# Where layer B's modulation vectors are summed, and how many root series a linear-attention head runs

## The chip, the cores and the metric

The kernel runs on one core of one Trainium2 chip. The metric is the time of one execution on the device in microseconds (us); of several runs the median is taken. Of the engines this text speaks of TensorE (PE), VectorE (DVE), ScalarE (ACT), GpSimd (POOL) and of the queue of DMA issues on SyncE (SP). Each engine works through its own instructions in a fixed order.

## The reference, cut to what matters

Two layers work on 1024 tokens of width 1024. Layer A is a gated delta rule with 8 heads of 128, layer B a stick-breaking attention with 16 heads of 64 over keys and values that are computed once between the layers. Every layer, and the keys and values too, read the tokens through a norm that is modulated by vectors from a condition `c`:

```python
def _modulated_norm(x, gain, shift, scale):
    n = _rms(x, gain) * (1.0 + scale[:, None, :]) + shift[:, None, :]
...
    o = _chunk_gated_delta(q, k, v, g, beta)
    o = _rms(o, o_gain) * jax.nn.silu(z)
...
    o = jnp.concatenate(outs, axis=2).transpose(0, 2, 1, 3).reshape(B, T, W)
    o = o * jax.nn.silu(z)
    return o.astype(h.dtype) @ w_out
```

For each layer a 1024x3072 matrix `w_ada` multiplies the activated `c` and gives shift, scale and a gate for the layer's output (parts 0, 1 and 2); a 1024x2048 matrix does the same for the keys and values (shift and scale). These are products of a matrix with one vector: little arithmetic, but 4 MB of weights for each part.

## The kernel before

**Stages.** From 0 to 80 us the kernel loads `x`, sums layer A's own shift and scale and projects the first heads. From 80 to some 680 us it runs layer A's 8 heads. The loop over heads (L748 to L775) emits for each head the projection and convolution of the next head's q and k, the finishing of a modulation part that is pending (`pend`), the values, the triangular solve, and `stage_c`, which runs the chunk recurrence and norms the output. The out-projection's first part begins at 640 us, its rest and the keys (`keys_values`, first half) run to 829.65 us, the values half from there to some 920 us, and layer B with its attention and out-projection to the end.

**Projections.** Each float32 weight tile is cast to a high part `whi` (ACT, L211), the rest `wlo` is taken by a subtract (DVE, L212), and three matmuls (L116 to L118) multiply high by high, high by low and low by high. These matmuls fill PE's order between everything else.

**Modulation vectors.** `mod_acc` (L145) sums a 512-wide half of a part: 8 loads of 256 KB from `w_ada` (SP, L151), and on DVE one product (L153) and 7 multiply-adds (L155) of 128x512, which leave a tile of 128 partial sums for each column. `mod_fin` (L170), in its turned form, transposes that tile on PE (four 128x128 transposes `pc` for a half, L182), sums each transposed block by an ACT instruction with accumulation (L185), adds the bias, and writes shift, scale or, after one more transpose `pr` (L202), the gate's row to memory. In the loop over heads the list `mods` (L527) gives each of the heads 0 to 5 one part: layer A's gate, scale and shift of the keys and values, then scale, shift and gate of layer B.

**The output's norm.** At the end of `stage_c` (L726 to L744) each half of the tokens has its own root series on DVE: a sum of squares by ACT, `qe`, `so`, then `rsqrt` (L96 to L101, 11 instructions on 128x4), a multiply of the 128x512 tile `osb`, four PE transposes `pto`, a multiply by the silu gate `sz`, and a store.

**Keys and values.** `kv_half` runs 16 times (8 blocks of columns n, two halves of the tokens), four steps each; a step is 24 matmuls of 128x256. n from 0 to 3 makes keys, n from 4 to 7 values, so the values half has 32 steps. After each n, `mod_b(n)` (L919) loads 128 rows of the normed tokens, applies layer B's scale and shift on ACT (L923), casts on DVE (L926) and subtracts on POOL (L927), which makes the tiles `hbT` that layer B's projections read.

**Order.** Up to the keys and values stage a scheduler orders all engines by its own plan. In the keys and values stage PE's order is that in which the code emits (`manual_schedule`, L947), and the other engines are still ordered by the scheduler. Loads are issued on SP in its order, and wait there for a free buffer.

Of the kernel before, what the change touches and what calls it, by code (L numbers as in the profile page):

```python
# [8 lines left out]
F32 = mybir.dt.float32  # L9
# [3 lines left out]
ALU = mybir.AluOpType  # L13
# [9 lines left out]
def kernel(  # L23
# [146 lines left out]
    def mod_fin(pool, ps_pool, ps_tag, i, part, accs, j0=0, turned=False):  # L170

        t = pool.tile([P, ND], F32, name="mt", tag="mt", bufs=2)
# [27 lines left out]
        else:  # L200
# [326 lines left out]
    mods = [(0, 2), (2, 1), (2, 0), (1, 1), (1, 0), (1, 2)]  # L527
# [160 lines left out]
    def stage_c(h, st):  # L688
# [37 lines left out]
        for hf in range(TH):  # L726
            cs = slice(hf * 4, hf * 4 + 4)
            osb = osbs[hf]
            so = gp.tile([P, 4], F32, name="so", tag="so")
            for i in range(4):  # L730
                sqo = gp.tile([P, P], F32, name="sqo", tag="sqo")
                S.activation(out=sqo, in_=osb[:, i], func=AF.Square, accum_out=so[:, i:i + 1])

            qe = gp.tile([P, 4], F32, name="qe", tag="qe")
            V.tensor_scalar(out=qe, in0=n2[:, 0, cs], scalar1=EPS, scalar2=EPS * P, op0=ALU.add, op1=ALU.mult)
            V.scalar_tensor_tensor(out=so, in0=so, scalar=1.0 / P, in1=qe, op0=ALU.mult, op1=ALU.add)
            ro = rsqrt(gp, so, 4, "ro")
            V.tensor_tensor(out=osb, in0=osb, in1=ro[:, :, None].broadcast_to([P, 4, P]), op=ALU.mult)
            pt = ch_pool.tile([P, 4, P], F32, name="pto", tag="ch")
            for i in range(4):  # L740
                PE.transpose(pt[:, i], osb[:, i], ident)
            V.scalar_tensor_tensor(out=szs[hf], in0=pt.rearrange("p a b -> p (a b)"), scalar=ogain,
                                   in1=szs[hf], op0=ALU.mult, op1=ALU.mult)
            dma(out=oTa[h, :, hf * 512:hf * 512 + 512], in_=szs[hf])  # L744
# [4 lines left out]
    for h in range(HA):  # L749
# [23 lines left out]
        if h < len(mods):  # L773
            i, part = mods[h]
            pend = (i, part, [mod_acc(gp, i, part, n0, 512, 2) for n0 in (0, 512)])  # L775
# [143 lines left out]
    def mod_b(n):  # L919
# [360 lines left out]
```

## Time and profile before

| | us |
|---|---|
| median of 3 runs | 1466.41 (1465.34 to 1467.45) |
| profiled execution | 1462.12 |
| its span, first to last instruction | 1460.3 |
| PE busy | 1374.8 |
| DVE busy | 1040.8 |
| ACT busy | 760.6 |
| POOL busy | 92.3 |

The profiled execution lies 4.3 us under the median, and 1.8 us of it are outside the span. PE's matmuls overlap and their ends are modelled, so a busy PE says only that something is queued; times at which PE sits idle and stretches at a lower granted clock say more. The granted clock is a share of 2.4 GHz; its lower level is 1.2 GHz.

### The profile page before, as it was taken

The numbers are of one execution on the slowest core, as the hardware profiler recorded it, in microseconds if no ns is written. First come the engines' busy times: TensorE is split into PE (matmuls) and PEld (weight loads), VectorE is DVE, ScalarE is ACT, GpSimd is POOL, SyncE is SP. The second block draws the span as 40 slices with busy tenths as digits, with TensorE's granted clock in tenths as the row PEclk, the third lists the DMA queues.
The fourth block names the chain that finished last, engine by engine and source line by source line (L and its number), as shares of the span: only waits on it lengthen the run. The fifth ranks groups of instructions, "written<-read, shape, count | busy, mean of one in ns | idle before, by whom it ended". The sixth has DMA issues, their size and how long they took to land.

```text
span 1460.3 us, 23391 instructions
## 1 busy us (share of the span) xinstructions
PE 1374.8 (94%) x8603; PEld 1145.8 (78%) x8603; DVE 1040.8 (71%) x2459; ACT 760.6 (52%) x1614; POOL 92.3 (6%) x98
## 2 busy tenths in 40 slices
PE   4989999799999999999799999999999999998998
PEld 3567778578878777788689999788888888885676
DVE  3568698878778788954886610488888888989332
ACT  5656546446564646431784422366666666665110
POOL 1000000000000000000221011301011011000000
PEclk9999999799999999999999999999999999999999
DMA  9334324443444444444844433624233233234511
GB/s 316 107 107 124 89 51 120 123 137 84 142 108 133 108 137 134 148 127 162 301 160 159 160 131 116 181 73 116 54 101 106 69 105 87 84 84 131 174 59 56
DMA packets 168132, 181.15 MB, mean 124 GB/s; under 512 B 36617, under 2 KB 121426, under 8 KB 168018
## 3 DMA queue, kind: packets, MB, share of 16 engines
q1 hardware_dynamic: 165184, 171.17, 39.4%
q0 software_dynamic: 2432, 8.39, 1.6%
q8 instruction: 68, 1.11, 0.3%
q14 instruction: 46, 0.38, 0.1%
q10 hardware_dynamic: 402, 0.10, 0.0%
HBM read 140.22 MB, written 39.40 MB: 123 GB/s over the span
## 4 chain that ended last, share of the span: by engine, by line
PE 70%; DVE 18%; ACT 6%; DMA 3%; issue 2%; SPq 0%; ACTq 0%; DVEq 0%
PE pj L116 16%; PE pj L117 16%; PE pj L118 16%; DVE kp L1074 3%; PE ptw L1089 3%; PE pa L1114 2%; PE pa L1115 2%; PE pl L1069 1%; PE pl L1068 1%; PE pgr L576 1%; DVE qk L515 1%; DVE wl L1096 1%; DVE macc L155 1%; DMA mraw<-in_w_ada_dram 1%; PE pa L1111 1%
## 5 line engine op out<-in xcount | busy, mean ns | idle before, releaser
L118 PE MATMUL pj<-hT,wlo 128*128 128x512 f32 x496 | 203.0, 410 | 10.2 <-DVE wlo L212 10.2
L116 PE MATMUL pj<-hT,whi 128*128 128x512 f32 x496 | 205.4, 414 | 3.7 <-ACT qk L513 2.6
L117 PE MATMUL pj<-hT,whi 128*128 128x512 f32 x496 | 204.5, 412 | 0.0
L1074 DVE TENSOR_TENSOR_SCAN kp<-kp,stick 128x896 f32<-128x896 f32 (+7 forms) x128 | 179.1, 1401 | 3.9 <-ACT kp L1070 2.6
L1070 ACT ACTIVATE kp<-pl,nrq 128x512 f32<-128x512 f32 (+1 forms) x192 | 107.0, 580 | 48.6 <-PE pl L1069 39.9
L1094 ACT ACTIVATE wh<-ptw 128x512 fp32r<-128x512 f32 (+3 forms) x152 | 84.6, 557 | 67.4 <-PE ptw L1089 63.2
L118 PEld LDWEIGHTS pj<-hT,wlo 128*128 128x128 f32 x496 | 95.2, 192 | 27.6 <-DVE wlo L212 11.8
L116 PEld LDWEIGHTS pj<-hT,whi 128*128 128x128 f32 x496 | 95.2, 192 | 24.2 <-issue 3.7
L116 PE MATMUL pj<-hbT,whi 128*128 128x512 f32 x256 | 108.0, 422 | 0.0
L117 PEld LDWEIGHTS pj<-hT,whi 128*128 128x128 f32 x496 | 95.3, 192 | 15.8
L116 PE MATMUL pj<-wo,oh 128*128 128x512 f32 x256 | 103.8, 405 | 4.0 <-ACT oh L254 2.3
L117 PE MATMUL pj<-wo,oh 128*128 128x512 f32 x256 | 102.1, 399 | 0.0
L118 PE MATMUL pj<-wo,ol 128*128 128x512 f32 x256 | 101.3, 396 | 0.5 <-DVE ol L255 0.5
L117 PE MATMUL pj<-hbT,whi 128*128 128x512 f32 x256 | 101.2, 395 | 0.0
L118 PE MATMUL pj<-hbT,wlo 128*128 128x512 f32 x256 | 101.2, 395 | 0.0
L1089 PE MATMUL ptw<-ident,kp 128*128 128x128 f32 x576 | 91.6, 277 | 8.1 <-DVE wl L1096 5.5
L212 DVE TENSOR_TENSOR wlo<-wraw,whi 128x1024 fp32r<-128x1024 f32 x56 | 68.7, 1226 | 39.8 <-ACT whi L211 35.5
L211 ACT CAST whi<-wraw 128x1024 fp32r<-128x1024 f32 x56 | 59.1, 1055 | 72.1 <-PE pj L117 61.0
L1096 DVE SCALAR_TENSOR_TENSOR wl<-ptw,wh 128x512 fp32r<-128x512 f32 (+1 forms) x140 | 87.3, 624 | 8.1 <-ACT wh L1094 7.2
L1089 PEld LDWEIGHTS ptw<-ident,kp 128*128 128x128 f32 x576 | 68.4, 142 | 27.3 <-DVE wl L1096 12.0
L1114 PE MATMUL pa<-wh,vt 128*128 128x256 f32 (+1 forms) x280 | 78.5, 302 | 10.6 <-DVE o L1131 10.6
L116 PE MATMUL pj<-whi,hkT 128*128 128x256 f32 x256 | 73.2, 286 | 2.4 <-DVE x L265 1.6
(324 smaller groups left out, 3428.8 us busy)
## 6 DMA issues: line engine op xcount, KB each, us to landing
mraw<-in_w_ada_dram SPq DMA_DIRECT2D x96, 256.0 KB
wraw<-in_w_in_a_dram SPq DMA_DIRECT2D x32, 512.0 KB
mraw<-in_w_ada_kv_dram SPq DMA_DIRECT2D x32, 256.0 KB
xr<-x_dram SPq DMA_DIRECT2D x16, 512.0 KB
wraw<-in_w_kv_dram SPq DMA_DIRECT2D x16, 512.0 KB
kT_dram<-kt SPq DMA_DIRECT2D x32, 256.0 KB
wraw<-in_w_in_b_dram SPq DMA_DIRECT2D x16, 512.0 KB
Kh<-kT_dram SPq DMA_DIRECT2D x32, 256.0 KB
```

The costliest lines, as they stand in the source:

```text
L116: PE.matmul(ps, lh, rh, start=start, stop=False)
L117: PE.matmul(ps, lh, rl, start=False, stop=False)
L118: PE.matmul(ps, ll, rh, start=False, stop=stop)
L211: (copy or S.copy)(out=hi, in_=raw)
L212: (eng or G).tensor_tensor(out=lo, in0=raw, in1=hi, op=ALU.subtract)
L1070: S.activation(out=kp[:, s0:s0 + sw], in_=pl[:, :sw], func=AF.Sigmoid, scale=nrq[p][:, t, e:e + 1])
L1074: V.tensor_tensor_scan(out=kr, data0=kr, data1=stick[:, T - n:][:, ::-1], initial=1.0, op0=ALU.mult, op1=ALU.max)
L1089: PE.transpose(pt[:, i], kps[p, e, 2 * g + q][:, j * P:(j + 1) * P], ident)
L1094: S.activation(out=wh[:, :nb], in_=pt[:, :nb], func=AF.Copy, bias=-1.0)
L1096: V.scalar_tensor_tensor(out=wl[:, :nb], in0=pt[:, :nb], scalar=-1.0, in1=wh[:, :nb], op0=ALU.add, op1=ALU.subtract)
L1114: PE.matmul(dst, lh, wh[:, sl], start=(j == 0), stop=False)
L1115: PE.matmul(dst, lh, wl[:, sl], start=False, stop=(j == nj - 1))
```

## The change

It has four parts.

1. `mods` is cut to layer A's gate and the keys' and values' scale and shift. Each of the heads 0 to 5 sums one half (8 DVE instructions, 8 loads) where it summed a whole part, and a part is finished after every second head.
2. Layer B's three parts are summed in the values half, in 12 quarters of 256 columns. A quarter (`mod_quarters`) has 4 loads of 256 KB into a ring of five buffers `x2k`, which the keys' tiles `kt` use as well, and 8 DVE instructions of 128x256. They are emitted at the steps of `MOD_Q`, and the column sums (two transposes `pc` on PE, two accumulations on ACT, small DVE rows) four steps later. The gate's transpose `pr` follows the last of them.
3. `mod_b` is emitted at the steps of `MOD_B`, where it followed each n, and its subtract moves from POOL to DVE.
4. `stage_c` runs one root series of 8 columns for both halves, in the heads 0 to 6; the last head keeps two.

```diff
+    def mod_quarters(pool, i, part):
+        for n0 in range(0, D, 256):
+            src = mod_src[i][:, part * D + n0:part * D + n0 + 256].rearrange("(p k) n -> p k n", k=8)
+            acc = pool.tile([P, 256], F32, name="macq", tag=("of", "oh", "ol")[n0 // 256 % 3], bufs=2)
+            for k in range(0, 8, 2):
+                raw = pool.tile([P, 2, 256], F32, name="mrawq", tag="x2k", bufs=5)
+                dma(out=raw, in_=src[:, k:k + 2])
+                for kk in range(2):
+                    if k + kk == 0:
+                        V.tensor_scalar(out=acc, in0=raw[:, 0], scalar1=cact[:, 0:1], scalar2=None, op0=ALU.mult)
+                    else:
+                        V.scalar_tensor_tensor(out=acc, in0=raw[:, kk], scalar=cact[:, k + kk:k + kk + 1], in1=acc,
+                                               op0=ALU.mult, op1=ALU.add)
+            yield acc, n0 // P
...
-    mods = [(0, 2), (2, 1), (2, 0), (1, 1), (1, 0), (1, 2)]
+    mods = [(0, 2), (2, 1), (2, 0)]
+    half_acc = []
...
-        for hf in range(TH):
-            cs = slice(hf * 4, hf * 4 + 4)
...
-            ro = rsqrt(gp, so, 4, "ro")
...
+        groups = [(0, 1)] if h < HA - 1 else [(0,), (1,)]
+        for group in groups:
...
+            ro = rsqrt(gp, so[:, ga], 4 * len(group), f"ro{len(group)}")
+            for hf in group:
...
-        if h < len(mods):
-            i, part = mods[h]
-            pend = (i, part, [mod_acc(gp, i, part, n0, 512, 2) for n0 in (0, 512)])
+        if h < 2 * len(mods):
+            i, part = mods[h // 2]
+            half_acc.append(mod_acc(gp, i, part, h % 2 * 512, 512, 2))
+            if h % 2:
+                pend, half_acc = (i, part, half_acc), []
...
-            G.tensor_tensor(out=hT[hf][:, 1, n], in0=xs, in1=hT[hf][:, 0, n], op=ALU.subtract)
+            V.tensor_tensor(out=hT[hf][:, 1, n], in0=xs, in1=hT[hf][:, 0, n], op=ALU.subtract)
...
+    def mods_b(step, made):
+        if quarters and quarters[0][0] + 4 <= step:
+            _, i, acc, j0 = quarters.pop(0)
+            mod_fin(kp_, wk_pool, "wk", 1, (1, 0, 2)[i], [acc], j0, tg if i == 2 else None, turned=True)
+        if step in MOD_Q:
+            n = MOD_Q.index(step)
+            quarters.append((step, n // 4, *next(made)))
...
+                    if n >= 4:
+                        mods_b(step, made)
+                        if step in MOD_B:
+                            mod_b(MOD_B.index(step))
+                        step += 1
...
-            mod_b(n)
...
+    MOD_Q = (0, 1, 3, 4, 6, 7, 9, 10, 16, 19, 22, 25)
+    MOD_B = (15, 16, 18, 19, 21, 22, 24, 26)
```

Three places show what it does to the engines' orders. DVE first, before, a piece of head 1's solve: `ttmp` and `tt` are the pair of small instructions that a row of the triangular solve takes, `macc` is the summing of a modulation part, `vv`, `Sn` and `so` belong to the head before.

```order
L606 TENSOR_TENSOR tt<-tt,ttmp 128x2x24
L709 TENSOR_SCALAR vv<-pw,b_1132 128x128
L603 TENSOR_TENSOR ttmp<-bf,tt 128x3x23
L155 SCALAR_TENSOR_TENSOR macc<-mraw,cact,macc 128x512
L606 TENSOR_TENSOR tt<-tt,ttmp 128x3x23
L717 SCALAR_TENSOR_TENSOR Sn<-Sn,gA_110,pS 128x128
L603 TENSOR_TENSOR ttmp<-bf,tt 128x3x22
L515 SCALAR_TENSOR_TENSOR qk<-xp,ccol,qk 128x1024
L606 TENSOR_TENSOR tt<-tt,ttmp 128x3x22
```

DVE, the same piece of head 1's solve in the changed kernel.

```order
L623 TENSOR_TENSOR tt<-tt,ttmp 128x2x24
L620 TENSOR_TENSOR ttmp<-bf,tt 128x3x23
L726 TENSOR_SCALAR vv<-pw,b_1132 128x128
L623 TENSOR_TENSOR tt<-tt,ttmp 128x3x23
L620 TENSOR_TENSOR ttmp<-bf,tt 128x3x22
L623 TENSOR_TENSOR tt<-tt,ttmp 128x3x22
L734 SCALAR_TENSOR_TENSOR Sn<-Sn,gA_110,pS 128x128
L620 TENSOR_TENSOR ttmp<-bf,tt 128x3x21
L228 TENSOR_TENSOR wlo<-wraw,whi 128x1024
```

Between the first `ttmp` of head 1 and the end of its solve the kernel before has 14 rows of `macc`; the changed kernel has none there, since the part's second half was summed earlier and the next part begins with head 2. A `wlo` row of the next weights, which stood behind the solve, now stands within it.

PE in the changed kernel, at step 29 of the values half (the steps count from 0), where the gate's last column sums are taken. `macq` is the last quarter, `tg` the gate's vector.

```order
L117 MATMUL pj<-kwl,hkT 128x256
L118 MATMUL pj<-kwh,hkT 128x256
L198 MATMUL pc<-ident,macq 128x128 x2
L218 MATMUL pr<-ident,tg 8x128
L116 MATMUL pj<-whi,hkT 128x256
L117 MATMUL pj<-wlo,hkT 128x256
```

Twelve such pairs `pc` now stand in the values half among the projections' matmuls, and this last one has `pr` right behind it, which reads what ACT and DVE make of the pair.

SP in the changed kernel, at the end of the keys half and the start of the values half. `kt` are tiles of keys that are stored, `mrawq` the quarters' loads, `wraw` weights of keys and values.

```order
L941 DMA kT_dram<-kt 128x512 x8
L177 DMA mrawq<-in_w_ada_dram 128x2x256 x5
L233 DMA wraw<-in_w_kv_dram 128x4x256
L177 DMA mrawq<-in_w_ada_dram 128x2x256
L233 DMA wraw<-in_w_kv_dram 128x4x256
L177 DMA mrawq<-in_w_ada_dram 128x2x256 x2
L941 DMA kT_dram<-kt 128x512 x3
```

The quarters' loads stand around the next weights' loads and around the last stores of keys, where the kernel before had the weights and the stores alone.

## Rows read from the trace of the kernel before

**Rows 1.** The page: busy time, share of the span, instructions

```profile
PE 1374.8 (94%) x8603; PEld 1145.8 (78%) x8603; DVE 1040.8 (71%) x2459; ACT 760.6 (52%) x1614; POOL 92.3 (6%) x98
```

**Rows 2.** Windows of layer A: stretch, its length, each engine's busy us, PEclk, DMA

```profile
core 0: us, PE busy (x) PEld busy (x) DVE busy (x) ACT busy (x) POOL busy (x), PEclk, DMA share, GB/s
...
256.00:284.00 28.00, 17.89 (x68) 12.83 (x67) 27.11 (x102) 12.81 (x32) 0.00 (x0) 0.70 0.47 129
284.00:373.00 89.00, 87.97 (x631) 71.15 (x630) 62.51 (x196) 50.80 (x134) 0.00 (x0) 1.00 0.43 117
...
460.00:484.00 24.00, 21.02 (x104) 17.11 (x103) 23.85 (x77) 17.99 (x36) 0.00 (x0) 0.93 0.51 148
...
514.00:560.00 46.00, 44.23 (x240) 36.33 (x240) 43.73 (x159) 24.75 (x55) 0.00 (x0) 1.00 0.43 129
```

**Rows 3.** Waits of PE from 256 to 284 us: total, times, longest

```profile
PE pj L118 <- DVE wlo L212: 5.4, 1, 5.4
PE pgr L576 <- ACT kdec L549: 3.2, 2, 1.6
```

**Rows 4.** Chain of waits from 254 to 284 us: start, length, what

```profile
254.80 0.66 DVE macc L155
...
259.16 3.02 DMA mraw<-in_w_ada_kv_dram
...
263.93 0.66 DVE macc L155
...
274.85 1.15 DVE wlo L212
276.04 0.79 PE pj L118
276.83 3.57 PE pgr L576 x8
280.40 0.43 PE pj L116
```

**Rows 5.** Instructions on the sums' tile: count, ns min/median/max, first and last start

```profile
L155 DVE SCALAR_TENSOR_TENSOR macc<-mraw,cact,macc x84: 735/744/755, 93.5 to 543.4; 128x512 f32<-128x512 f32 x84
...
L182 PE MATMUL pc<-ident,macc x48: 270/272/330, 221.6 to 572.2; 128*128 128x128 f32 x48
L185 ACT ACTIVATE macc<-pc x48: 268/278/331, 222.2 to 573.3; 128x128 f32<-128x128 f32 x48
...
L153 DVE TENSOR_SCALAR macc<-mraw,cact x12: 472/481/487, 91.9 to 529.5; 128x512 f32<-128x512 f32 x12
```

**Rows 6.** Timeline of PE around one group of column sums: start, length

```profile
221.31 0.40 PE L118 MATMUL pj<-hT,wlo 128*128 128x512 f32 x1
221.55 0.60 PE L182 MATMUL pc<-ident,macc 128*128 128x128 f32 x4
221.91 0.48 PE L116 MATMUL pj<-hT,whi 128*128 128x512 f32 x1
222.22 0.40 PE L117 MATMUL pj<-hT,whi 128*128 128x512 f32 x1
```

**Rows 7.** Windows of the values half

```profile
840.00:860.00 20.00, 20.00 (x173) 20.00 (x173) 3.65 (x5) 5.85 (x10) 2.66 (x2) 1.00 0.49 162
860.00:880.00 20.00, 20.00 (x173) 20.00 (x172) 2.35 (x4) 5.73 (x10) 3.63 (x2) 1.00 0.38 116
```

**Rows 8.** Windows of the two stretches with the highest DMA rate

```profile
0.00:20.00 20.00, 4.71 (x16) 2.99 (x17) 8.02 (x32) 13.04 (x21) 4.17 (x20) 1.00 0.90 323
700.00:720.00 20.00, 14.94 (x76) 11.90 (x75) 17.68 (x43) 18.57 (x46) 6.47 (x9) 0.91 0.96 335
```

**Rows 9.** Groups of DVE instructions from 80 to 700 us: busy us, mean ns

```profile
L587 DVE TENSOR_TENSOR qk<-qk,gb 128x512 f32<-128x512 f32 x16 | 10.9, 682 | 0.0
...
L101 DVE SCALAR_TENSOR_TENSOR ro_y<-ro_z,ro_y 128x4 f32<-128x4 f32 x48 | 7.5, 156 | 0.4
```

**Rows 10.** Issues of the sums' loads on SP

```profile
L151 SPq DMA_DIRECT2D mraw<-in_w_ada_dram x64: 327/328/702, 82.0 to 539.9; - x64
```

More of the change, by code (lines that the diff above doesn't have):

```diff
@@ L168, in mod_rows, with mod_fin @@
         return row
-    def mod_fin(pool, ps_pool, ps_tag, i, part, accs, j0=0, turned=False):
-        t = pool.tile([P, ND], F32, name="mt", tag="mt", bufs=2)
+    def mod_quarters(pool, i, part):
[12 more added lines that the diff above has]
+            yield acc, n0 // P
+    def mod_fin(pool, ps_pool, ps_tag, i, part, accs, j0=0, t=None, turned=False):
+        t = t if t is not None else pool.tile([P, ND], F32, name="mt", tag="mt", bufs=2)
         nj = accs[0].shape[1] // P
@@ L199, in mod_fin @@
                                    op0=ALU.add, op1=ALU.mult)
-        else:
+        elif js.stop == ND:
             pr = ps_pool.tile([P, 512], F32, name="pr", tag=ps_tag)
@@ L724, in stage_c @@
             osbs.append(osb)
-        for hf in range(TH):
-            cs = slice(hf * 4, hf * 4 + 4)
[L728 to L736, printed above, removed]
-            ro = rsqrt(gp, so, 4, "ro")
[L738 to L744, printed above, removed]
@@ new lines, in stage_c @@
+        so = gp.tile([P, NC], F32, name="so", tag="so")
+        qe = gp.tile([P, NC], F32, name="qe", tag="qe")
+        groups = [(0, 1)] if h < HA - 1 else [(0,), (1,)]
+        for group in groups:
+            ga = slice(group[0] * 4, group[-1] * 4 + 4)
+            for hf in group:
+                for i in range(4):
+                    sqo = gp.tile([P, P], F32, name="sqo", tag="sqo")
+                    S.activation(out=sqo, in_=osbs[hf][:, i], func=AF.Square, accum_out=so[:, hf * 4 + i:hf * 4 + i + 1])
+            V.tensor_scalar(out=qe[:, ga], in0=n2[:, 0, ga], scalar1=EPS, scalar2=EPS * P, op0=ALU.add, op1=ALU.mult)
+            V.scalar_tensor_tensor(out=so[:, ga], in0=so[:, ga], scalar=1.0 / P, in1=qe[:, ga], op0=ALU.mult,
+                                   op1=ALU.add)
+            ro = rsqrt(gp, so[:, ga], 4 * len(group), f"ro{len(group)}")
+            for hf in group:
+                osb = osbs[hf]
+                r = ro[:, (hf - group[0]) * 4:(hf - group[0]) * 4 + 4]
+                V.tensor_tensor(out=osb, in0=osb, in1=r[:, :, None].broadcast_to([P, 4, P]), op=ALU.mult)
+                pt = ch_pool.tile([P, 4, P], F32, name="pto", tag="ch")
+                for i in range(4):
+                    PE.transpose(pt[:, i], osb[:, i], ident)
+                V.scalar_tensor_tensor(out=szs[hf], in0=pt.rearrange("p a b -> p (a b)"), scalar=ogain,
+                                       in1=szs[hf], op0=ALU.mult, op1=ALU.mult)
+                dma(out=oTa[h, :, hf * 512:hf * 512 + 512], in_=szs[hf])
@@ L926, in mod_b, with sums_of_mods @@
             V.tensor_copy(out=hT[hf][:, 0, n], in_=xs)
-            G.tensor_tensor(out=hT[hf][:, 1, n], in0=xs, in1=hT[hf][:, 0, n], op=ALU.subtract)
+            V.tensor_tensor(out=hT[hf][:, 1, n], in0=xs, in1=hT[hf][:, 0, n], op=ALU.subtract)
+    tg = kp_.tile([P, ND], F32, name="tg", bufs=1)
+    quarters = []
+    def sums_of_mods():
+        for part in (1, 0, 2):
+            yield from mod_quarters(kp_, 1, part)
+    def mods_b(step, made):
[5 more added lines that the diff above has]
+            quarters.append((step, n // 4, *next(made)))
     def keys_values():
-        parts, tail = kv_weights(0), None
+        parts, tail, made, step = kv_weights(0), None, sums_of_mods(), 0
         yield
```

## The prediction

> **What bounds the kernel now.** I began with the page's busy times: PE is busy for 94% of the span and DVE for 71% [rows 1]. So most of the time is PE's, and work taken from DVE is worth something only where PE waits for DVE. The windows of layer A show where that is [rows 2]. From 284 to 373 us PE is busy for 87.97 of 89 us, DVE for 62.51: less DVE work gives nothing there. From 256 to 284 us it is the other way round: DVE 27.11 of 28 us, PE 17.89, and the granted clock is 0.70, so some of the stretch ran at 1.2 GHz, the lower level. From 460 to 484 us there is a smaller place of the kind, with PE at 21.02 of 24 and a clock of 0.93, and from 514 to 560 us PE lacks 1.77 us. The waits name the releaser: one wait of 5.4 us for `wlo`, which DVE makes, and 3.2 us for `kdec`, which ACT makes from what DVE gives it [rows 3]. The chain of waits goes through DVE's queue from 254.80 to 276 us: five pieces of `macc` (the first at 254.80, the last at 263.93, each 0.66), a wait of 3.02 us for a load `mraw` in between, then at 274.85 the `wlo` for which PE waits [rows 4]. The sums of modulation parts are on the path there.
>
> The values half looks the other way. PE is busy for 20.00 of 20 us, DVE for 3.65 and 2.35, and the DMA engines for 0.49 and 0.38 of their time [rows 7]. DVE and the queues have room, and PE has none: each instruction that is put into PE's order there costs its whole length.
>
> **Part by part.** *DVE work that leaves layer A.* 96 instructions sum there now, 84 of 0.744 us and 12 of 0.481 [rows 5], and half of them go: 42 x 0.744 + 6 x 0.481 = 34 us. Besides, one root series of 8 columns takes the place of two of 4: with `qe` and `so`, 13 of 156 ns from start to end [rows 9] in layer A's loop leave for each of seven heads, about 1 us a head when they follow each other at some 0.075 us. Most of that hides under PE and is worth nothing. What counts:
>
> The first wall, 256 to 284 us. PE is idle for 28 - 17.89 = 10.1 us, and the matmuls that run at the lower clock cost more: 8 `pgr` in 3.57 us, of which half is lost, 1.8, and the `pj` at 0.43 us [rows 4] against the 0.23 from start to start at full clock [rows 6], 0.2 each for four or five of them, 0.9. At most 10.1 + 2.7 = 12.8 us can come back. From the order: in head 1's solve 14 `macc` leave, at 0.66 us each by the chain's pieces 9.2 us, and 1 us of root rows; in their place an `e` row and some `nm` rows move in, some 2.5 us. So DVE's part gets 7.7 us shorter. At the low end the clock falls all the same and other waits take 2 us of it: 6. I take 10, since a DVE queue that is 7.7 us shorter leaves only some 2.5 us of idle time, nearer to the second wall, where 3 us of idle time cost a clock of only 0.93 [rows 2]. What is late next is PE's own queue.
>
> The second wall, 460 to 484 us: 24 - 21.02 = 3.0 us idle and about 1 us of clock. Half of the `macc` of that head leaves, 8 x 0.66 = 5.3 us, and I take 3, with 1 and 4 as bounds. 514 to 560 us and short waits elsewhere: 1.77 us idle; I take 1.5, bounds 0 and 3.
>
> *PE work that leaves layer A.* A group of four transposes lets the next matmul start 221.91 - 221.55 = 0.36 us later, and the one behind it 0.31 after that where 0.23 is the rule [rows 6]: 0.44 us. Three parts have six groups: 2.6 us, and `pr` once, 0.2: 2.8 in all (2.5 to 3). The ACT accumulations, 24 of 0.278 [rows 5], lie beside PE's work. Layer A together: -10 - 3 - 1.5 - 2.8 = **-17.3 us** (-9.5 to -23).
>
> *PE work that enters the values half.* 12 pairs of transposes. Two transposes less than a group leave 0.44 - 0.22 = 0.22 us at the lowest, a whole group's 0.44 is the highest; I take 0.33: 4.0 us (2.6 to 5.3). The last pair has `pr` right behind it in an order that is fixed. PE must wait for the pair's end, 0.27 [rows 5], two accumulations of 0.28 with their reads of the sum, some 0.2 each, 1.0 together, and the bias row on DVE, some 0.16 by the small rows [rows 9], before `pr` can run, itself as long as one of the pair, 0.27: 1.2 to 2.0 us with nothing ahead on ACT, and up to 4 if a cast of 1 us or two is queued there. I take 1.8. Together **+5.8 us** (3.8 to 9.3).
>
> *DVE, SP and POOL in the values half.* 84 multiply-adds and 12 products of 128x256: by the line through 156 ns for 4 columns and 744 for 512 [rows 5, 9] about 0.45 us each, 42 us; 16 subtracts of 0.68 [rows 9], 11 us. DVE uses 3.65 us of 20 [rows 7], so 53 us in 90 fit. The sums stand before `wlo` and `kwl` rows in DVE's queue, and a late load holds those up; the weights' ring is a whole n, 22 us, ahead. Without this cover each late row would cost PE its lateness. 48 issues on SP at 0.33 us [rows 10] are 16 us. `mod_b` moved later still ends before 911 us by its last step, 26; PE needs `hbT` from some 920. POOL loses its 16 subtracts, for which nobody waits there. All this at nothing, if the loads come in time; that is the first rival.
>
> Sum: -17.3 + 5.8 = **-11.5 us**, from the profiled 1462.1 to 1450.6. The profiled run lies 4.3 us under the median; on the median that is 1466.4 - 11.5 = **1455**.
>
> **Rivals.** *The values half becomes bound by its loads (slower).* A step is 24 matmuls, at 173 in 20 us [rows 7] 2.78 us. Eight quarters, 8 x 4 x 256 KB = 8.4 MB, must be summed before PE reaches the transposes of the eighth, after 15 steps and 7 pairs: 43.4 us from the half's start. Other traffic in that time is 139 GB/s by the mean of the windows [rows 7], 6 MB, less 1 MB of `mod_b` loads that move out. 13.4 MB in 43.4 us are 310 GB/s, just under the two highest stretches of the trace, 323 and 335 [rows 8]. So it can go wrong. At 280 GB/s the eighth quarter comes 4.5 us late, at 250 10 us, and PE, in a fixed order, waits for all of it; the saving of 11.5 is gone at 244 GB/s, and below some 232 the kernel is slower by over 3 us; at 225 it stands at 1471. For it: five buffers, on which stores of keys wait too. Against it: with 3.02 us for a load [rows 4] and 0.9 for its two DVE rows five buffers turn over 1.3 MB in 3.9 us, 335 GB/s, where the quarters ask for 195; and the sums may start before the half does, since the order has five loads ahead of it. The Trainium skill's page "DMA: Bandwidth & Descriptors", section "Anatomy of one DMA — SWDGE (gpsimd) path", gives some 2.0 us for each transfer and its bytes at 436 GB/s besides, so by my estimate from it 13.4 MB take 31 us and this rival falls away, with the sum as it stands; the trace's highest windows of 323 and 335 GB/s do not reach that rate, and the page's fit is of another issuing queue. Chance 0.12, most of it slower.
>
> *The wall only moves.* Layer A's orders come from a plan. If the joint root series, whose second half must wait for the first's squares and whose `pto` come together, or the earlier `wlo` row put another wait in front of PE, the first wall gives 3 instead of 10 and the second nothing: -3 - 1.5 - 2.8 + 5.8 = -1.5, 1465, no measurable change. For it: the wall's chain also has `vT`, `qk`, `n` and `sz` rows, which stay. Against it: DVE's whole load falls in the very stretch in which it is full. Chance 0.10.
>
> *The wall goes altogether,* and the clock with it: -12.8 - 4 - 3 - 3 = -22.8, + 5 for the values half: -17.8, 1449. Chance 0.13.
>
> **How the numbers follow.** The forecast has 0.65. A difference of 0.2%, 2.9 us, is about what a measurement tells from no change. Two of its larger terms at their far ends give 1450 and 1463, all of them at once 1447 and 1466; the first rival reaches past 1469. The range 1446 to 1466 takes in all but the worse half of the first rival and what no bound here covers. Faster takes the forecast, the third rival and a little of the second: 0.80. Same: most of the second and the mild end of the first: 0.11. Slower: the rest of the first: 0.09.
>
> **What would show it.** Right: the stretch from the first `ttmp` of head 1 to its end with PE idle for under 4 us, and a granted clock near 1.00; layer A shorter by 14 to 20 us; in the values half PE without idle time but for one wait of 1 to 2 us before `pr`, and the half longer by about 6. Wrong: waits of `pc` for `macq` with a DMA as releaser behind them, or a DMA share under 0.9 while they last (then the ring, not the rate, binds); a wait of PE for `wlo` or `osb` of 5 us in another head; `hbT` later than PE's first read of it.

## The result and the profile after

| | us |
|---|---|
| kernel before, median of 4 runs | 1466.93 (1465.34 to 1469.04) |
| changed kernel, median of 4 runs | 1448.68 (1445.75 to 1453.10) |
| ratio, 95% interval | 0.988 (0.986 to 0.990) |
| profiled execution before / after | 1462.12 / 1449.83 |
| span before / after | 1460.3 / 1448.1 |

The kernel got 18 us faster by the medians and 12.3 by the profiled executions. The forecast was 11.5 us and 1455, and the time lies within the range, nearer to its low end than to the forecast.

The busy times of the changed kernel, from its page; [rows 1] is the line of before.

```profile
PE 1372.3 (95%) x8603; PEld 1145.0 (79%) x8603; DVE 1061.1 (73%) x2447; ACT 766.3 (53%) x1616; POOL 69.7 (5%) x82
```

The four windows of layer A after the change, to lay beside [rows 2] (columns as there).

```profile
256.00:284.00 28.00, 28.00 (x179) 22.83 (x179) 26.20 (x97) 20.46 (x60) 0.00 (x0) 1.00 0.32 85
284.00:373.00 89.00, 87.63 (x607) 70.46 (x607) 67.94 (x212) 49.01 (x107) 0.00 (x0) 1.00 0.36 102
...
460.00:484.00 24.00, 24.00 (x142) 19.40 (x142) 20.62 (x70) 14.77 (x35) 0.00 (x0) 1.00 0.33 84
...
514.00:560.00 46.00, 45.30 (x221) 37.01 (x220) 33.99 (x97) 27.58 (x71) 0.00 (x0) 1.00 0.40 121
```

Both walls are gone. Between 256 and 284 us PE was busy for 17.89 us with 68 matmuls at a clock of 0.70; now for 28.00 with 179 at 1.00. Between 460 and 484 it has no idle time either. The changed kernel's heads begin earlier by then, so these are not the same pieces of work; by pieces of work, from the first `pw` (the recurrence's product with the solved block) of head 4 to that of head 5, PE's idle time went from 3.4 us to 0.0.

Where stages begin can be read from the first start of their matmuls. First before, then after: `pj<-hT` is layer A's first projection, `pj<-whi,hkT` the first of keys, `pj<-hbT` the first of layer B (the times are the first and the last start).

```profile
L116 PE MATMUL pj<-hT,whi x496: 387/393/988, 43.9 to 588.0; 128*128 128x512 f32 x166
...
L116 PE MATMUL pj<-whi,hkT x256: 276/278/562, 713.5 to 918.6; 128*128 128x256 f32 x128
...
L116 PE MATMUL pj<-hbT,whi x256: 388/397/628, 920.4 to 1319.3; 128*128 128x512 f32 x128
```

```profile
L116 PE MATMUL pj<-hT,whi x496: 387/393/796, 48.6 to 567.0; 128*128 128x512 f32 x166
...
L116 PE MATMUL pj<-whi,hkT x256: 276/276/562, 694.3 to 909.0; 128*128 128x256 f32 x128
...
L116 PE MATMUL pj<-hbT,whi x256: 387/397/481, 910.8 to 1307.1; 128*128 128x512 f32 x128
```

So layer A (43.9 to 713.5, now 48.6 to 694.3) takes 645.6 us where it took 669.5: 23.9 less. Keys and values together take 9.7 us more. The values half alone, from its first matmul (the 769th of 1536 on `hkT`) to the first on `hbT`, takes 100.1 us where it took 90.9: 9.2 more. The changed kernel's profiled execution also began layer A 4.7 us later, in code that is the same: it ran at the lower clock for 6.8 us from 31 us on and again from 45 on, the one before for 3.4 us once. That is not the change's doing: c1_z2_pool, which has the code of the kernel before up to there, also took 47.9 us. It is 4.7 of the 6 us that lie between 18 by the medians and 12.3 by the profiles. The table has these lengths for every kernel of this study, worked out from the traces in the same way (us; "to A" is the time to the first projection):

| profiled execution of | to A | layer A | keys half | values half | layer B | span |
|---|---|---|---|---|---|---|
| before | 43.9 | 669.5 | 116.0 | 90.9 | 539.9 | 1460.3 |
| the changed kernel | 48.6 | 645.6 | 116.5 | 100.1 | 537.3 | 1448.1 |
| a1_two_roots | 46.5 | 641.7 | 118.8 | 101.1 | 537.2 | 1445.3 |
| a2_no_sums | 45.8 | 648.7 | 116.6 | 92.4 | 535.9 | 1439.5 |
| a3_no_loads | 46.9 | 648.7 | 121.6 | 94.4 | 539.2 | 1450.8 |
| a4_dense | 48.3 | 649.1 | 116.3 | 102.2 | 541.0 | 1457.0 |
| b1_one_root | 44.5 | 655.8 | 119.6 | 90.9 | 536.8 | 1447.6 |
| b2_dense_two | 48.1 | 648.4 | 116.3 | 102.2 | 536.6 | 1451.6 |
| b3_late_sums | 48.1 | 645.2 | 119.3 | 100.5 | 537.8 | 1450.8 |
| b4_spread | 48.4 | 646.0 | 116.9 | 102.0 | 538.3 | 1451.7 |
| c1_z2_pool | 47.9 | 664.4 | 116.6 | 90.9 | 537.3 | 1457.1 |
| c2_hold | 45.0 | 646.5 | 118.2 | 103.6 | 537.2 | 1450.6 |
| c3_late_dve | 46.1 | 647.7 | 116.9 | 101.8 | 538.0 | 1450.4 |
| c4_spread_dve | 48.9 | 646.9 | 116.9 | 102.9 | 537.7 | 1453.3 |

The table also shows how far chance goes: seven of these have the changed kernel's layer A unaltered (the changed one, a2, a3, b3, b4, c3, c4), and it took 645.2 to 648.7 us. A difference of 3 us in a stage of one execution says little.

One name has to be put right before the experiments. What the text ahead calls head 1's solve is the third in the trace, that of head 2; it runs beside the recurrence of head 1. Rows and times there are those of this solve.

### The profile page after: what moved, and what is told of

It reads as the page before. It is cut to its first block, busy times and chain, and to the rows that moved or that the text cites. A ratio compares the mean times of both kernels' runs of the same rounds, so it can differ in the third digit from the quotient of the medians.

```text
span 1448.1 us, 23372 instructions
## 1 busy us (share of the span) xinstructions
PE 1372.3 (95%) x8603; PEld 1145.0 (79%) x8603; DVE 1061.1 (73%) x2447; ACT 766.3 (53%) x1616; POOL 69.7 (5%) x82
## 4 chain that ended last, share of the span: by engine, by line
PE 70%; DVE 16%; DMA 6%; ACT 5%; issue 2%; SPq 0%; ACTq 0%; DVEq 0%
PE pj L116 16%; PE pj L117 15%; PE pj L118 15%; DVE kp L1121 4%; PE ptw L1136 3%; DMA mrawq<-in_w_ada_dram 2%; PE pa L1161 2%; PE pa L1162 2%; PE pgr L593 2%; PE pl L1116 2%; PE pl L1115 1%; DVE macq L182 1%; DVE wl L1143 1%; PE pw L724 1%; PE po L736 1%
## 5 line engine op out<-in xcount | busy, mean ns | idle before, releaser
L118 PEld LDWEIGHTS pj<-hT,wlo 128*128 128x128 f32 x496 | 94.4, 190 | 16.4
```

The costliest lines, as they stand in the source:

```text
L118: PE.matmul(ps, ll, rh, start=False, stop=stop)
```

## The experiments

### What made the first wall

The theory of the prediction: DVE has too much to do around 256 us, and the 14 sums of 128x512 are what counts of it. The first runs took the parts of the change one from another.

**a1_two_roots** keeps the change and gives every head two root series.

```diff
-        groups = [(0, 1)] if h < HA - 1 else [(0,), (1,)]
+        groups = [(0,), (1,)]
```

> The changed kernel with two root series in every head again (part 4 undone, all else kept). Theory: layer A's gain is the sums that left DVE's queue in the solves of heads 1 and 4; the root series are 13 short DVE rows a head, about 1 us, and only where PE waits for DVE does that count. 1 to 3 us slower than the changed kernel, layer A (first layer-A projection to first key projection) longer by 1 to 3. Rival: the joint series is what keeps the first wall away, since its rows stood in the chain; then 8 us or more slower, with a wait of PE for wlo near 270 us.

Measured: 1447.32 us, ratio to the kernel before 0.985 (0.982 to 0.987), and the changed kernel's is 0.988 (0.986 to 0.990). Layer A took 641.7 us, not longer. With the sums moved, the joint series is worth nothing that can be measured. The rival falls, and the theory's 1 to 3 us with it.

**a4_dense** keeps the change, but the three parts that stay in layer A are summed whole in heads 0 to 2, so that the third solve has its 14 sums again.

```diff
-        if h < 2 * len(mods):
-            i, part = mods[h // 2]
-            half_acc.append(mod_acc(gp, i, part, h % 2 * 512, 512, 2))
...
+        if h < len(mods):
+            i, part = mods[h]
+            pend = (i, part, [mod_acc(gp, i, part, n0, 512, 2) for n0 in (0, 512)])
```

> The changed kernel with the three parts that stay in layer A summed as whole parts in heads 0 to 2, as before, and none in heads 3 to 5. The same number of sums leaves layer A. Theory: what counts is which solve has the sums in it: the wall of head 1 comes back with 16 sums in its stretch, the one of head 4 does not; 8 to 16 us slower than the changed kernel. Rival: only the total matters (24 us of loads, PE transposes and DVE time less): within 3 us of the changed kernel.

Measured: 1455.12 us, 0.991 (0.989 to 0.993), layer A 649.1. The wall did not come back: the window of 256 to 284 us has PE busy for 27.02 us, and its one wait for a `wlo` there is 1.0 us.

```profile
256.00:284.00 28.00, 27.02 (x138) 22.20 (x137) 27.76 (x101) 13.47 (x31) 0.00 (x0) 1.00 0.54 144
```

DVE is as full as it was before (27.76 of 28 us, [rows 2] has 27.11), the solve took 36.1 us from its first row to its last where it took 34.6 before, and yet PE hardly waits. The theory of the prediction, that DVE's load by itself makes the wall, doesn't survive this run. Neither size that was expected came: by the ratios the kernel is 0.3% slower than the changed one, and layer A, at 649.1, holds 3.5 us of that at most.

**b1_one_root** is the kernel before with part 4 alone: all sums and `mod_b` where they were, one root series in heads 0 to 6 (the lines of the change in `stage_c`, nothing else).

> The kernel before with part 4 alone: one root series for both halves in heads 0 to 6, all sums where they were. The solve of head 1 keeps its 14 sums on DVE. Theory, after the runs so far (14 sums in that solve with the joint series: no wall; none with two series: no wall either): the first wall takes both, and each relief is enough by itself; it goes here too, PE is idle for under 4 us between 256 and 290 us, and layer A gets 10 to 17 us shorter. Rival: the sums make the wall, and the joint series saves 1 us a head at best: 1 to 4 us.

Measured: 1447.70 us, 0.987 (0.984 to 0.989). The one small part gives the whole gain of the change. Layer A took 655.8 us, 13.7 less than before, and the values half its old 90.9. The window:

```profile
256.00:284.00 28.00, 27.14 (x195) 21.65 (x194) 25.51 (x91) 12.63 (x31) 0.00 (x0) 1.00 0.52 146
```

The 14 sums are still in the solve, which took 35.4 us. The plan ordered many rows of the solve anew. The one that PE waited for in the kernel before is a row that no part of the change touches: the low part `wlo` of the weights of head 2's silu gate. In the kernel before it stands on DVE behind the whole solve and two rows of `vT`, and starts at 274.77 [rows 4]. Here it stands within the solve, as the timeline of DVE shows (start, length):

```profile
259.57 0.68 DVE L546 TENSOR_REDUCE n<-sq 128x4 f32<-128x512 f32 x1
260.17 0.22 DVE L606 TENSOR_TENSOR tt<-tt,ttmp 128x66 f32<-128x66 f32 x1
260.30 1.22 DVE L212 TENSOR_TENSOR wlo<-wraw,whi 128x1024 fp32r<-128x1024 f32 x1
261.44 0.22 DVE L603 TENSOR_TENSOR ttmp<-bf,tt 128x60 f32<-128x60 f32 x1
261.57 0.75 DVE L155 SCALAR_TENSOR_TENSOR macc<-mraw,cact,macc 128x512 f32<-128x512 f32 x1
```

**b2_dense_two** puts a4's whole parts together with a1's two series: the sums and series around the third solve are those of the kernel before.

> The changed kernel with whole parts in heads 0 to 2 and two root series in every head: head 1's solve has its 14 sums and two series as in the kernel before, heads 3 to 5 have none. Theory: with both the first wall is back: a wait of PE for wlo of 3 us or more near 275, a lower clock there, layer A 10 us longer than with whole parts and the joint series. Rival: the wall hangs on where the plan puts a wlo row or on the loads, and stays away; within 3 us.

Measured: 1455.86 us, 0.992 (0.990 to 0.994), layer A 648.4. The rival was right for layer A: no wall, PE busy for 25.56 of 28 us in the window, and 0.4 us of waiting for a `wlo`. The same work stands on DVE as in the kernel before, in another order. The starts of that one row, from the traces, beside the time at which PE first multiplies by it (the solve goes from the start of its first `tt` row to that of its last):

| kernel | solve, from to | `wlo` of head 2's gate | PE uses it |
|---|---|---|---|
| before | 236.1 to 270.7 | 274.8, behind the solve | 276.0 |
| b1_one_root | 235.8 to 271.1 | 260.3, within | 261.6 |
| a4_dense | 240.4 to 276.5 | 265.5, within | 266.8 |
| b2_dense_two | 239.4 to 277.3 | 263.6, within | 265.1 |
| a1_two_roots | 239.2 to 265.5 | 247.9, within | 266.0 |
| the changed kernel | 239.4 to 266.0 | 246.0, within | 265.1 |

**c1_z2_pool** tests this place by itself on DVE. It is the kernel before with that one subtract on POOL; up to the end of the solve every other row of DVE stands where it stood. PE's order did change: the plan now puts matmuls of this gate among the transposes and `pgr` from 264 us on, where the kernel before starts no projection matmul between 261.30 and 276.04.

```diff
-                wz.extend(split_w(load_w(w_in_a[0][:, (24 + h) * P:(25 + h) * P]), [P, ND, P], None, V))
+                wz.extend(split_w(load_w(w_in_a[0][:, (24 + h) * P:(25 + h) * P]), [P, ND, P], None,
+                                  G if h == 2 else V))
```

> The kernel before with one subtract moved: the low part wlo of the weights of head 2's silu gate (L212, called from silu_z) is made on POOL. Sums, root series and DVE's order in the solve that runs from 240 to 271 us stay row for row. Place theory: in the kernel before this one row stands on DVE behind the whole solve, at 274.77, and PE wants it near 262 to 265; in every other kernel run so far it stands within the solve, and none has the wall, whatever sums or series it has. So the wall goes: PE idle under 4 us from 256 to 284, no lower clock there, layer A 10 to 15 us shorter, kernel 1452 to 1458. Load theory (the one of the prediction): DVE's queue is as full as before and the chain's other rows are as late; at most 3 us.

Measured: 1460.46 us, 0.995 (0.993 to 0.997); layer A 664.4, 5.1 less than before. The window, and PE's waits for `wlo` in layer A:

```profile
256.00:284.00 28.00, 25.27 (x125) 20.21 (x126) 27.71 (x112) 12.74 (x30) 0.00 (x0) 0.98 0.47 126
```

```profile
PE pj L118 <- DVE wlo L212: 4.0, 2, 2.7
```

The place accounts for most of the idle time in the window: 28 - 25.27 = 2.7 us are left of 10.1, and the clock there went from 0.70 to 0.98. The 3.2 us of PE's waits for `kdec` [rows 3] are gone as well, as they are in b1 and a4 (b2 has 0.2). But only a part of the gain reaches the end of layer A. DVE's later rows are still late: both waits for a `wlo` lie behind the window, 2.7 us between 300 and 360 and 1.3 between 360 and 440, where the kernel before has 0.5 in all. From one head's first `pw` to the next one's, heads 1 to 2 take 7.2 us less, 2 to 3 and 3 to 4 take 2.9 and 1.4 more, 4 to 5 take 5.7 less and 6 to 7 take 4.9 more; why the last two changed was not tested. Neither theory had the size of 5.1: the place theory said 10 to 15 us for layer A, the load theory at most 3.

**c2_hold** is the opposite test. In the changed kernel the same row is made to wait for the solve: it multiplies by a one that is taken from the solve's last row.

```diff
+                    one = gp.tile([P, 1], F32, name="one")
+                    V.tensor_scalar(out=one, in0=st["tt"][:, 0, 31:32], scalar1=0.0, scalar2=1.0, op0=ALU.mult,
+                                    op1=ALU.add)
...
+                    V.scalar_tensor_tensor(out=lo, in0=raw, scalar=one, in1=hi, op0=ALU.mult, op1=ALU.subtract)
```

> The changed kernel with the same row held back: the low part of head 2's gate weights multiplies by a one that is made from the solve's last row, so DVE can't make it before the solve's end. Sums and series as in the changed kernel. Place theory: PE waits for it, some 3 us or more, and the clock may fall after it: layer A 4 to 12 us longer than in the changed kernel. Load theory: with 14 sums gone from the solve DVE comes to the row in time; within 2 us.

Measured: 1453.91 us, 0.990 (0.988 to 0.993); layer A 646.5 beside 645.6. The held row costs PE one wait:

```profile
PE pj L118 <- DVE wlo L650: 1.5, 1, 1.5
```

The solve, with no sums in it, took 25.4 us and ended at 260.9, the row ran at 261.5, PE used it at 262.8. So the load theory holds here: within 2 us. (The 5 us between this median and the changed kernel's do not come from layer A; the values half took 103.6 us in this execution.)

All these kernels can be laid side by side in the stretch from head 1's first `pw` to head 2's. The plan puts different numbers of projection matmuls there, 0.23 us each [rows 6], so these are taken off:

| kernel | sums in the solve | the row | stretch | `pj` in it | the rest |
|---|---|---|---|---|---|
| before | 14 | behind | 71.6 | 148 | 37.6 |
| c1_z2_pool | 14 | on POOL, early | 64.4 | 158 | 28.1 |
| b1_one_root | 14 | within | 64.7 | 180 | 23.3 |
| a4_dense | 14 | within | 65.4 | 180 | 24.0 |
| b2_dense_two | 14 | within | 68.6 | 187 | 25.6 |
| c2_hold | none | behind | 57.9 | 151 | 23.2 |
| a1_two_roots | none | within | 61.5 | 172 | 21.9 |
| the changed kernel | none | within | 56.3 | 151 | 21.6 |

So the wall needs both, a row of the next weights that the plan puts behind the solve, and a solve that is 8 to 12 us longer for the 14 sums in it. Take the sums out and the row's place costs 1.6 us of the stretch. Move the row alone and 9.5 of 16 us go; let the plan order the rest anew as well (b1, a4, b2) and 12 to 14 go, with all sums in place. The joint series, two series in another form, whole or half parts: each of them made the plan put the row within the solve. Why the plan does so is not to be seen in a trace and stays open.

### What the values half costs

**a2_no_sums** leaves layer B's sums out: constants stand for its scale, shift and gate.

```diff
+    V.memset(mod_gs[1], 1.0)
+    V.memset(mod_sh[1], 0.0)
...
-                        mods_b(step, made)
```

> The changed kernel without layer B's sums: no loads, no DVE sums, no column sums, no gate transpose; layer B's scale, shift and gate are constants, so its output is another one. mod_b stays at its steps. Theory: the values half goes from 100.0 us back to 90.8, so 9 us less than the changed kernel, and the ACT wait for the xhl loads no longer holds up the kv copies. Rival: a part of the 9 us belongs to mod_b's new places (its loads come in threes and ACT waits for them); then the half stays at 92 or more and the gain is 7 or less.

Measured: 1441.51 us, 0.982 (0.980 to 0.984); values half 92.4. So 7.7 of the 9.2 us are the sums', and 1.5 belong to `mod_b`'s new places: PE waits 1.3 us for a `kv` copy of ACT even without the sums. The rival has a part of the truth.

**a3_no_loads** sums over the resident tokens in place of `w_ada`.

```diff
-                raw = pool.tile([P, 2, 256], F32, name="mrawq", tag="x2k", bufs=5)
-                dma(out=raw, in_=src[:, k:k + 2])
+                raw = hkT[:, 0, k, :512].bitcast(F32).rearrange("p (k n) -> p k n", k=2)
```

> The changed kernel with the quarters' DVE sums taken over a resident tile (the first key weights' partner, the modulated tokens) in place of w_ada: same DVE and PE work, the 48 loads left out, so the output is another one. Theory: what the pairs cost in PE's order stays (12 x 0.33 = 4.0 us and 1.1 for the gate's transpose), what late loads cost goes: waits of the pairs for sums (3.5 us) and of the kv copies behind xhl (1.8): values half 95 us, 4 to 5 us faster than the changed kernel. Rival: PE's order and DVE's time alone make the 9 us: no change, half still 99 to 100.

Measured: values half 94.4 us, 5.7 less than with the loads, as expected; of PE's waits there, only the one before the gate's transpose is left. The whole kernel took 1451.85 us, 0.988 (0.986 to 0.990), no less than the changed one. The run takes away more than the loads: with nothing to wait for, 48 of the 96 rows of sums ran beside the keys, the first at 699.57, so half of DVE's work left the half too. The keys half paid for it. It took 121.6 us where the changed kernel's took 116.5, and PE waited there for a row of the keys' norm on DVE:

```profile
PE pk L935 <- DVE kv L931: 4.1, 1, 4.1
```

The 5.7 us are therefore what the loads and their waits cost together with half of the sums' DVE rows, and the whole time is no measure of the loads.

So the half's 9.2 us split into 12 pairs of transposes, 0.22 to 0.23 us each (worked out below), 2.7; the gate's `pr` with the wait before it, 1.2; and a remainder of 5.3. Of this remainder the trace of the changed kernel shows 4.2 as waits, of two forms: late sums, 2.7, and `kv` copies, 1.5. PE's waits from 810 to 911 us:

```profile
PE pc L198 <- DVE macq L182: 2.7, 3, 1.8
PE pj L116 <- ACT kv L913: 1.5, 2, 1.3
PE pr L218 <- DVE tg L209: 1.0, 1, 1.0
```

The first is the rival of the prediction: late sums. PE's timeline at the worst of them:

```profile
847.35 0.28 PE L118 MATMUL pj<-kwh,hkT 128*128 128x256 f32 x1
849.40 0.44 PE L198 MATMUL pc<-ident,macq 128*128 128x128 f32 x2 [1.78 <-DVE macq L182]
849.60 0.36 PE L116 MATMUL pj<-whi,hkT 128*128 128x256 f32 x1
```

The second was not foreseen. ACT's timeline (in brackets the idle time before a row and what ended it):

```profile
867.67 0.37 ACT L913 COPY kv<-pj 128x256 f32<-128x256 f32 x1 [2.43 <-PE pj L118]
871.58 2.60 ACT L947 ACTIVATE xhl<-xhl,sh,gs 128x1024 f32<-128x1024 f32 x2 [3.54 <-DMA xhl<-xhT_dram]
874.09 0.35 ACT L913 COPY kv<-pj 128x256 f32<-128x256 f32 x1
```

ACT waits 3.54 us for `mod_b`'s load, then runs two of its rows, and only then copies the projection `kv` out of PSUM, for which PE waits. `mod_b` now loads in the time in which the quarters do: windows of 10 us show the DMA engines at 0.96, 0.94 and 1.01, and the first 50 us together at 0.91.

```profile
810.00:860.00 50.00, 47.17 (x401) 46.36 (x400) 38.84 (x92) 14.82 (x52) 0.00 (x0) 1.00 0.91 280
...
810.00:820.00 10.00, 10.00 (x89) 10.00 (x88) 8.45 (x17) 3.63 (x8) 0.00 (x0) 1.00 0.96 309
...
830.00:840.00 10.00, 9.90 (x86) 9.69 (x85) 8.67 (x22) 4.27 (x13) 0.00 (x0) 1.00 0.94 283
840.00:850.00 10.00, 7.61 (x64) 7.21 (x63) 8.75 (x22) 1.83 (x8) 0.00 (x0) 1.00 0.83 241
850.00:860.00 10.00, 9.66 (x84) 9.46 (x83) 6.47 (x18) 1.84 (x11) 0.00 (x0) 1.00 1.01 307
```

The worst of the late sums falls into the window of 840 to 850, at 0.83 and 241 GB/s: there the DMA engines were not full. SP, which issues the quarters' loads, waited in these 50 us for DVE to give buffers of the ring back:

```profile
SPq L177 <- DVE macq L182: 12.2, 17, 2.1
```

### Four tries for a cheaper values half

**b3_late_sums** takes the column sums six steps after a quarter and the gate's transpose behind the half's last matmul.

```diff
-        if quarters and quarters[0][0] + 4 <= step:
+        if quarters and quarters[0][0] + 6 <= step:
...
         next(tail, None)
+        gate_row(kp_, wk_pool, "wk", 1, tg)
```

> The changed kernel with the column sums six steps after a quarter, not four, and the gate's transpose behind the last matmul of the values half. Theory: the waits of the pairs for late sums (3.5 us) and the 1.1 us before the gate's transpose go, the pairs' own 4.0 and the kv copies behind xhl (1.5 to 1.8) stay: values half 96 us, 4 us less than in the changed kernel. Rival: later pairs push the loads behind them as far, since the ring frees no sooner: half 99 or more.

Measured: 1450.37 us, 0.988 (0.984 to 0.991); half 100.5. The pairs wait no more, nor does `pr`, but PE now waits 4.4 us in one piece for a `kv` copy. ACT behind its load again:

```profile
862.76 1.24 ACT L951 ACTIVATE xhl<-xhl,sh,gs 128x1024 f32<-128x1024 f32 x1 [7.91 <-DMA xhl<-xhT_dram]
863.91 0.62 ACT L917 COPY kv<-pj 128x256 f32<-128x256 f32 x2
```

After the stall PE ran for some 5 us at the lower clock, 0.21 us from matmul to matmul where 0.12 is the rule. What the pairs gave back went there. The half came out at the rival's 99 or more, but not for the rival's reason, later loads.

**b4_spread** asks for the quarters at an even rate: scale and shift in turns, one every two steps, `mod_b` as soon as its columns are there. The column sums come five steps after a quarter, and the gate's transpose last.

```diff
...
-    MOD_Q = (0, 1, 3, 4, 6, 7, 9, 10, 16, 19, 22, 25)
-    MOD_B = (15, 16, 18, 19, 21, 22, 24, 26)
+    MOD_Q = (0, 2, 4, 6, 8, 10, 12, 14, 16, 18, 21, 24)
+    MOD_B = (9, 11, 13, 15, 17, 19, 21, 23)
```

> The changed kernel with the quarters spread over the half: scale and shift in turns, one quarter every two steps, column sums five steps later, mod_b as soon as its two columns are there (steps 9 to 23), the gate's quarters last and its transpose behind the last matmul. The same work, asked for at an even rate: 12 quarters in 24 steps. Theory: loads come in time and the DMA share falls from over 0.9 to about 0.8, no wait of a pair for its sum, less waiting of ACT for xhl: values half 95 us, 5 us less than in the changed kernel. Rival: more loads beside mod_b's and the weights': waits of the kv copies behind xhl grow, half 98 or more.

Measured: 1449.06 us, 0.988 (0.986 to 0.991); half 102.0. No pair waits, and the `kv` copies do, four times, 6.2 us in all, the longest 3.6. The rival was right.

**c3_late_dve** and **c4_spread_dve** are these two with `mod_b`'s scale and shift on DVE.

```diff
-        S.activation(out=xh, in_=xh, func=AF.Identity, scale=mod_gs[1][:, n:n + 1], bias=mod_sh[1][:, n:n + 1])
+        V.tensor_scalar(out=xh, in0=xh, scalar1=mod_gs[1][:, n:n + 1], scalar2=mod_sh[1][:, n:n + 1], op0=ALU.mult,
+                        op1=ALU.add)
```

> The kernel with column sums six steps later and the gate's transpose at the end, and with mod_b's scale and shift on DVE in place of ACT. Theory: what held PE up in that kernel was ACT, which waited for xhl with the kv copies queued behind it (4.6 us and a lower clock after it); with DVE waiting instead, nothing that PE needs at once is behind it. Values half 95 us (90.9 and 12 pairs of 0.33), against 100.1 in the changed kernel. Rival: DVE's wait delays the sums or the weights' low parts by as much; half 99 or more.

> The kernel with the quarters spread evenly, and with mod_b's scale and shift on DVE in place of ACT. Theory: the four waits of 0.9 to 3.9 us behind xhl go, half 95 us, whole kernel 4 to 6 us under the changed one, if nothing else in it is disturbed. Rival: the loads stand in a queue that is too full in any order and the waits go to the pairs; half 98 or more.

Measured: 1449.80 us, 0.987 (0.983 to 0.992), half 101.8; and 1453.96 us, 0.990 (0.987 to 0.992), half 102.9. Both expectations failed, and in the same way. In c4 PE waits 7.1 us in one piece for a `kv` copy, behind a cast for which ACT waits 10.22. In c3 PE has one wait in the half:

```profile
PE pj L116 <- ACT kv L917: 6.0, 1, 6.0
```

and ACT stands before another row that waits for a load, the cast of the last weights:

```profile
869.50 0.37 ACT L917 COPY kv<-pj 128x256 f32<-128x256 f32 x1 [2.43 <-PE pj L118]
878.25 1.04 ACT L231 CAST whi<-wraw 128x1024 fp32r<-128x1024 f32 x1 [8.37 <-DMA wraw<-in_w_kv_dram]
...
880.63 0.64 ACT L917 COPY kv<-pj 128x256 f32<-128x256 f32 x2
```

The weights were issued at 870.24, behind the quarters and `mod_b`'s loads on SP. In both pairs of runs, with `mod_b`'s row taken away, the next row in ACT's order that needed a late load held up the copies. No try beat the changed kernel, and none got the half under 100 us while it had all its loads.

## Why the prediction was right, and where its steps were not

**The sign, the place and the range were right.** Layer A got shorter at the two walls that [rows 2] show, the values half longer by what enters PE's order, and 1448.7 lies in 1446 to 1466. By the profiled executions the forecast of 11.5 was 0.8 us off, but that is two errors and a chance cancelling: layer A gave 23.9, not 17.3; the half cost 9.2, not 5.8; the changed kernel's profiled execution lost 4.7 us before layer A, and layer B, which does the same work, took 2.6 less. By its own signs the prediction missed on both stages: it wanted layer A shorter by 14 to 20 us and the half longer by about 6. That the sum still fell into the range is in part luck.

**The first wall was priced too low, and its cause was wrong.** "I take 10", with 12.8 as the most: from the first `pw` of head 1 to that of head 2 the trace has 71.6 us before and 56.3 after, 15.3 less for about the same work (148 and 151 `pj`). The bound was made of PE's idle time and of the half-speed matmuls on the chain; the 68 matmuls that the window held, against 179 after, would have told that a PE that is busy for 17.89 us there does less than 17.89 us of work: between 265 and 282 us the granted clock was 0.50, the lower level. The step that failed is the next one: "in head 1's solve 14 `macc` leave" and with them the wall. Its arithmetic came out: the solve got 8.0 us shorter (34.6 to 26.6) where the sum had 7.7. But a4, b1 and b2 kept 14 sums there and had no wall, and b1 took away none in all of layer A and had the whole gain in time. What PE waited longest for, 5.4 of the 10.1 us, is one row behind the solve [rows 3, 4], and the two orders have it in different places. (`kdec`, another 3.2 us, ACT makes from PE's transposes `ptk`, and not, as the prediction reads it, from what DVE gives.) The text ahead says that it moved; the prediction gave the move no price, and its second rival took the earlier row for a risk.

**The second wall** gave some 6 us of PE's losses and not 3: the stretch from the first `pw` of head 4 to that of head 5 is 9.5 us shorter, 3.6 us of which is work that now stands elsewhere. The cause given for it, "Half of the `macc` of that head leaves", did not happen. The plan put both halves of a part beside the same solve, so 13 rows of `macc` stand within that of head 5 (422.0 to 463.7 us), where 14 did before (444.9 to 492.8). What moved is again a `wlo`. In the kernel before, DVE starts it at 477.56 us and PE waits for it (lines of the timelines of DVE and PE):

```profile
477.56 1.22 DVE L212 TENSOR_TENSOR wlo<-wraw,whi 128x1024 fp32r<-128x1024 f32 x1
...
478.83 0.50 PE L118 MATMUL pj<-hT,wlo 128*128 128x512 f32 x1 [2.98 <-DVE wlo L212]
```

In the changed kernel the same row, counted among the `wlo` rows from the start, begins at 448.68, and PE first multiplies by it at 464.92 without a wait:

```profile
448.68 1.22 DVE L228 TENSOR_TENSOR wlo<-wraw,whi 128x1024 fp32r<-128x1024 f32 x1
...
464.92 0.39 PE L118 MATMUL pj<-hT,wlo 128*128 128x512 f32 x1
```

No run moved this row alone, so here the cause is argued and not shown.

**The pairs were priced a little high.** At a pair that waits for nothing, the last matmul ahead of it starts at 825.51 and the second one behind it 0.46 us later, where two intervals of 0.12 would stand without the pair, so 0.22 to 0.23 each and 2.7 in all. That is the low bound; the middle, 4.0, was taken. **The gate's transpose** runs 1.24 us after the pair's second, so it costs 1.2, again at the low bound, where 1.8 was taken.

**"All this at nothing, if the loads come in time"** failed: they did not. The first rival came true at its mild end. The need was worked out as 310 GB/s (with the prediction's own 0.33 us a pair the time is 43.9 us and the need 305) and held against 323 and 335 [rows 8]. From 810 to 860 us the rate was 280 GB/s, for which the rival had the eighth quarter 4.5 us late; 2.7 us of late pairs were measured. The sums did not start before the half, as the rival's discussion hoped: their loads stand behind eight stores of keys on SP, and the first was issued at 810.76, where the half's first matmul starts at 810.71. And part of it was not the rate: in the window of the worst late pair the share was 0.83, under the 0.9 that the prediction named as the sign of the ring. What the working left out is who else waits in that time: `mod_b` was priced by its end ("before 911 us") and by DVE's room, not by ACT's queue, where its row waits for a load with the `kv` copies behind it. a2 and b3 show that price, 1.3 and 4.4 us in one wait.

**The rivals.** The wall that only moves did not come about in the changed kernel; c1 shows something of it, with 4.0 us of waits for `wlo` further on. The wall that goes altogether is what happened, at a chance of 0.13: its layer A was 22.8 us shorter, and 23.9 were measured, but its values half cost 5 us and the measured one 9.2, so that its 1449 agrees with the median in part by chance.

**What the change amounts to.** The joint root series alone (b1, 0.987), the moved sums alone (a1, 0.985) and both together (0.988) can't be told apart. The moved sums make layer A some 10 us shorter than b1's and give 9.2 back in the values half. The cheapest way to the same time is part 4 by itself.

## What to carry to other kernels

When an engine waits, look for the row that it waits for and for its place in the other engine's order before counting that engine's load: a row that the next stage needs can stand behind a long chain that it has nothing to do with, and any edit that reshuffles a planned order may cure it and take the credit. A run that takes one thing away can let other work move: look at the neighbouring stages before the difference is put down to that one thing. Test each part of a change alone, the smallest too. Before loads are put into a stretch where PE has no slack, list every row there that waits for a load and what stands behind it on its engine; a copy that frees PSUM behind such a row is a wait of PE.

## What the runs showed of the hardware

- In windows filled mostly by the quarters' loads, whose rows are of 1 KB, the DMA engines moved 307 GB/s at a share of 1.01 and 309 at 0.96. From 870 to 880 us, with no quarter's load issued between 869.28 and 879.45, they moved 311 at 0.90, and from 700 to 720 us of the kernel before 335 at 0.96 [rows 8]: the rate at a full share was not one number here.
- Half a width is more than half the time on DVE: the multiply-add of 128x256 took 485 ns where that of 128x512 takes 744 [rows 5], the product took 353 where 481.
- A subtract of 128x1024 took 2.38 us on POOL (c1) and 1.21 to 1.22 on DVE.
- The stretches at the lower clock fall differently in executions of the same code: "to A" went from 43.9 to 48.9 us, the keys half from 116.0 to 119.6 (a3, whose DVE work there is another, left out).
